# Order of 256- and 512-column products in an MLP's up blocks, and a last norm with a shorter root and paired stores

## The chip, the cores and the metric

One core of one Trainium2 chip. The metric is the device time of one execution in microseconds, as the median of several runs. The engines are TensorE (PE, with its weight loads shown as PEld), VectorE (DVE), ScalarE (ACT), GpSimd (POOL) and SyncE (SP), which mainly issues DMAs.

## The reference

One layer of a hybrid block over 512 latent tokens of width 2048 (with 256 context tokens ahead of the scans), all in float32. After two groups of recurrent heads and an output projection, the tokens pass through an RMSNorm, a SwiGLU MLP with a depthwise 3x3 convolution on its gate branch, a gated residual, and a final RMSNorm:

```
u = h @ w_up;  u_gate, u_val = split(u)          # 2048 -> 2 x 5504
g = conv3x3_depthwise(u_gate on an 8 x 64 grid) + conv_b
x = x + gt2 * ((silu(g) * u_val) @ w_down)       # 5504 -> 2048
out = x * rsqrt(mean(x*x) + eps) * g_final
```

## The kernel before, in words

Tokens lie in the free dimension (512 columns), channels in 128 partitions: x is 16 tiles of 128 x 512. Products at full accuracy are made of two float32r halves: a tensor is split into a high half (ScalarE casts, L90) and a low half (VectorE subtracts, L91), and high x high, high x low and low x high are added up in PSUM.

The MLP's 5504 channels are 43 tiles f of 128. The first four go through a plain product (up_two); the other 39 go through up_seven (L1207), which computes the two up products of a tile with seven block products in place of eight, a Strassen-like scheme over halves of the weights' 16 input tiles, gate and value, and left and right halves of the tokens. Each of the seven block products (product, L1226) has its own weight block, 128 x 1024, that is split into wh and wl, and eight input tiles k as operand, whose high and low halves of 256 tokens lie side by side. For each k there are two matmuls on TensorE: a **low product** of wl with the 256 columns of the operand's high half, and a **512-column product** of wh with both halves at once. In the kernel before, the eight low products of a block come first, and then the eight 512-column products:

```
for k in range(KH):
    mm(o[:, 0, :], wl[:, cs[k]], operands[n](k)[:, 0], start=first and k == 0, stop=False, ...)
for k in range(KH):
    mm(o, wh[:, cs[k]], operands[n](k), start=False, stop=k == KH - 1, ...)
```

The tiles wl rotate through two buffers (pool wlo), the tiles wh through three. The order of instructions on an engine follows the program order, except that the parts under tc.high_priority() are moved forward, the splits among them; each engine's queue is then worked off in order. Between the sixth and the seventh block product most tiles f also run one block of the down projection (down_block, L1298): 48 matmuls of 512 columns, whose result is added to x in DRAM by an accumulating DMA. Meanwhile VectorE and ScalarE do the splits, the sums of the scheme, and the convolution (nine taps, L1168 and L1170).

The end (from L1311): x is read back as 16 tiles x2[k]. For the first 12 of them the last down products are added (residual, L1041), the tile is squared (square, L1049, for the two parts of the tokens apart) and scaled by g_final on ScalarE (L1331). The last four tiles, k = 12 to 15, come by parts of the tokens: part 0 is tokens 0 to 383, part 1 is tokens 384 to 511. For each part: four down products, four residuals, four squares, then token_rstd (L1055): matmuls with a column of ones add up the squares over the channels (L1061), a mean with eps (L158) and rsqrt (L148) make 1/root on 128 x 3 or 128 x 1 numbers, and matmuls with the identity (L1068) spread them over all partitions into a PSUM tile r3, which ScalarE copies to SBUF as r3s (L1359). square adds the squares of several tiles on VectorE into one tile (L87), except for the last ones, which it keeps as tiles of their own (own): the last four where the part has 512 tokens (the norm behind the output projection), otherwise the last two. The small PSUM tiles of token_rstd come from a pool of two buffers (psB).

Finally, for each part and each k, x2[k] is multiplied by 1/root: k below 12 with k % 3 == 2 on GpSimd with r3s (L1369), the others on VectorE with r3, k of 12 and more with g_final in the same instruction (L1367). Each result is stored at once by a DMA of its own (L1373): part 0 from SP's queue, part 1 alternately from SP's and ScalarE's. The multiplications of part 1 have high priority.

token_rstd with rsqrt serves the norm behind the output projection too (four columns, before up_two).

Of the kernel before, what the change touches and what calls it, by code (L numbers as in the profile page):

```python
# [18 lines left out]
P = 128  # L19
D = 2048  # L20
# [50 lines left out]
def block_kernel(ctx: ExitStack, tc: tile.TileContext, a: dict, out: bass.AP):  # L71
# [11 lines left out]
    def mul(o, x, y):  # L83
        V.tensor_tensor(out=o, in0=x, in1=y, op=ALU.mult)
# [31 lines left out]
    msk = keep.tile([P, len(LEVELS), P], U8, name="msk")  # L116
    csil = keep.tile([P, 128], F32, name="csil")[:, 0:KT]
    modc = {n: keep.tile([P, KT], F32, name=f"mod{n}") for n in (2, 3, 4, 5)}
    wraw = pool(ctx, "wraw", 4)
    whi = pool(ctx, "whi", 2)  # L120
    wlo = pool(ctx, "wlo", 2)
# [26 lines left out]
    def rsqrt(v, t, o):  # L148

        S.activation(t, v, AF.Ln)  # L150
        S.activation(o, t, AF.Exp, scale=-0.5)
        mul(t, o, o)
        mul(t, t, v)
        V.tensor_scalar(out=t, in0=t, scalar1=-0.5, scalar2=1.5, op0=ALU.mult, op1=ALU.add)
        mul(o, o, t)

    def mean_eps(v, ps, n):
        V.tensor_scalar(out=v, in0=ps, scalar1=1.0 / n, scalar2=EPS, op0=ALU.mult, op1=ALU.add)  # L158
# [896 lines left out]
    def token_rstd(sums, pl, name, n=T):  # L1055

        nj = n // P
        ps = psb(f"ps_{name}", (P, nj))
        for i, sq in enumerate(sums):
            for j in range(nj):  # L1060
                PE.matmul(ps[:, j : j + 1], sq[:, P * j : P * j + P], cst[:, C_ONE : C_ONE + 1],  # L1061
                          start=(i == 0 and j == 0), stop=(i == len(sums) - 1), skip_group_check=True)
        var, scr, r = (pl.tile([P, nj], F32, name=f"{t}_{name}", tag=t) for t in ("rs1", "rs2", "rs3"))
        mean_eps(var, ps, D)
        rsqrt(var, scr, r)
        o = psb(f"rb_{name}", (P, n))
        for j in range(nj):
            PE.matmul(o[:, P * j : P * j + P], r[:, j : j + 1].to_broadcast([P, P]), ident, start=True, stop=True)  # L1068
        return o
# [137 lines left out]
    def up_seven(f):  # L1207
# [30 lines left out]
        def rows(x):  # L1238
# [103 lines left out]
    for pt, sl in enumerate(parts):  # L1342
        w = sl.stop - sl.start
        accs = [acc(f"dl{pt}_{i}", (P, w)) for i in range(4)]
        for i in range(4):
            c = slice(P * i, P * i + P)
            for n, (wh, wl, raw) in enumerate(wd):
                if pt == 0:
                    gh, gl = gs[fs[n]]
                    mm3(accs[i], wh[:, c], wl[:, c], gh[:, sl], gl[:, sl], n == 0, n == len(fs) - 1)  # L1350
                else:
                    mm(accs[i], raw[:, c], glast[:, n, :], start=(n == 0), stop=(n == len(fs) - 1))
        with tc.high_priority():
# [5 lines left out]
            S.copy(r3s, r3)  # L1359
        roots.append((r3, r3s))  # L1360
    for pt, sl in enumerate(parts):
        r3, r3s = roots[pt]
        with tc.high_priority() if pt else nullcontext():
            for k in range(KT):
                xx = x2[k][:, sl]
                if k >= 12:
                    V.scalar_tensor_tensor(out=xx, in0=xx, scalar=gnf[:, k : k + 1], in1=r3, op0=ALU.mult, op1=ALU.mult)  # L1367
                elif k % 3 == 2:
                    G.tensor_tensor(out=xx, in0=xx, in1=r3s, op=ALU.mult)  # L1369
# [3 lines left out]
                eng.dma_start(out[k, :, sl], xx)  # L1373


def arrange(x, c, ctx, c_ctx, w_mod, b_mod, g_norm1, g_norm2, w_in, gla_w_lr, gla_b_lr, mlstm_b_gate,
# [72 lines left out]
```

## Time and profile before

| what | value |
|---|---|
| median of 3 runs | 2485.04 us (2484.53 to 2485.16) |
| the profiled execution | 2483.26 us, of which the span is 2481.4 us |
| instructions | 35224 |
| TensorE busy | 98% of the span |
| VectorE, ScalarE, GpSimd busy | 71%, 45%, 15% |
| mean DMA rate | 173 GB/s |
| mean granted TensorE clock | 0.992 |

The profile is of one execution, so its own time stands beside the median. It has a page (busy time of the engines, shares of the chain of work that ended last, the costliest groups of instructions) and views that can be asked for a stretch: instructions in order of time, the chain in order of time, waits, DMAs, and busy time by stretches. In a row of the timeline the first number is the start in us from the span's beginning, the second the time that the group took; then come engine, line, operation, output<-input, shape and count, and in brackets the idle time of the engine before and what ended it. A row of the chain has start, time and what ran. A row of the stretches has the stretch, its length, busy time (and count) of PE, PEld, DVE, ACT and POOL, the granted clock, the DMA engines' share and GB/s. Matmuls are pipelined, and their ends are modelled, so two that follow one another overlap in the listing.

### The profile page before, as it was taken

What the parts mean: (1) busy time and instruction counts of PE and PEld (TensorE: products, weight loads), DVE (VectorE), ACT (ScalarE), POOL (GpSimd) and SP (SyncE); (2) the same over time, 40 slices, a digit from 0 to 9 for tenths busy, and PEclk for the clock granted to TensorE, in tenths of its full rate; (3) what the DMA queues carried; (4) which work ended last, traced back from release to release, by engine and by line L of the source; (5) the groups of instructions that cost most, each with busy time, mean ns of one, the idle gap of its engine ahead of it and who ended that gap; (6) DMA issues with size and microseconds to landing.
All of it is one profiled execution on the core that took longest, in us unless ns stands there. A gap on an engine that the chain in (4) does not pass through costs nothing.

```text
span 2481.4 us, 35224 instructions
## 1 busy us (share of the span) xinstructions
PE 2441.4 (98%) x13588; PEld 2107.1 (85%) x13588; DVE 1751.1 (71%) x2482; ACT 1113.2 (45%) x1652; POOL 367.4 (15%) x364
## 2 busy tenths in 40 slices
PE   7999999999999999999999999999999999999997
PEld 5888899888988888888888888888888888888886
DVE  5666766554545688777887777777777777777874
ACT  4224543322223444434455555555555555555552
POOL 0000000000000344540011111111111111111100
PEclk9999999999999999998999999999999999999998
DMA  9751012123433778862488888888888888888761
GB/s 380 270 190 57 33 38 78 63 93 125 136 132 102 266 267 293 280 196 90 144 187 191 192 191 198 193 191 192 190 193 188 187 193 190 191 190 191 177 202 68
DMA packets 138167, 429.66 MB, mean 173 GB/s; under 512 B 15760, under 2 KB 20240, under 8 KB 138000
## 3 DMA queue, kind: packets, MB, share of 16 engines
q1 hardware_dynamic: 104880, 348.24, 41.9%
q0 software_dynamic: 31968, 78.66, 19.7%
q8 instruction: 106, 1.74, 0.3%
q10 hardware_dynamic: 1152, 0.52, 0.1%
q14 instruction: 61, 0.50, 0.1%
HBM read 381.22 MB, written 46.14 MB: 172 GB/s over the span
## 4 chain that ended last, share of the span: by engine, by line
PE 95%; DVE 2%; DMA 1%; issue 1%; ACT 0%; SPq 0%; DVEq 0%; ACTq 0%
PE dn L98 18%; PE a L98 18%; PE x L98 17%; PE v L98 9%; PE wo L98 7%; PE ga L98 7%; PE w L98 4%; PE po L98 4%; PE u L98 4%; PE ps_m L98 1%; PE sl L98 1%; PE dl L98 1%; PE cst L98 1%; PE s L98 1%; PE mc L309 1%
## 5 line engine op out<-in xcount | busy, mean ns | idle before, releaser
L91 DVE TENSOR_TENSOR lo_q<-q,hi_q 128x1024 fp32r<-128x1024 f32 x195 | 235.4, 1223 | 142.6 <-ACT spare L1303 117.6
L90 ACT CAST hi_q<-q 128x1024 fp32r<-128x1024 f32 x195 | 205.2, 1052 | 230.0 <-PE dn L98 162.0
L98 PE MATMUL dn<-gh,lo_d 128*128 128x512 f32 x660 | 257.5, 390 | 0.0
L98 PE MATMUL dn<-gl,hi_d 128*128 128x512 f32 x660 | 257.5, 390 | 0.0
L98 PE MATMUL dn<-gh,hi_d 128*128 128x512 f32 x660 | 257.4, 390 | 0.0
L1170 DVE SCALAR_TENSOR_TENSOR cv<-pad,cwt,cv 128x512 f32<-128x512 f32 x328 | 246.7, 752 | 6.3 <-ACT cv L1168 0.5
L98 PE MATMUL x<-bt,hi_q 128*128 128x512 f32 x936 | 235.4, 394 | 0.0
L98 PEld LDWEIGHTS x<-bt,hi_q 128*128 128x128 f32 x936 | 167.6, 188 | 30.7
L1211 POOL DMA_DIRECT2D spare<-in_w_up x78 | 68.7, 884 | 720.0 <-DMA spare<-in_w_up 637.5
L298 POOL TENSOR_TENSOR sumg_m<-sumg_m,raw_m 128x512 f32<-128x512 f32 x74 | 124.1, 1677 | 199.3 <-ACT raw_m L297 170.7
L98 PE MATMUL a<-hi_h,hTh 128*128 128x256 f32 x512 | 150.3, 294 | 0.0
L91 DVE TENSOR_TENSOR lo_d<-raw_d,hi_d 128x1024 fp32r<-128x1024 f32 x84 | 101.3, 1206 | 65.8 <-ACT hi_d L90 51.4
L290 DVE SCALAR_TENSOR_TENSOR sum_m<-raw_m,csil,sum_m 128x512 f32<-128x512 f32 x112 | 145.5, 1299 | 1.3
L98 PEld LDWEIGHTS dn<-gl,hi_d 128*128 128x128 f32 x660 | 124.0, 188 | 26.2 <-DVE gl L91 0.2
L98 PEld LDWEIGHTS dn<-gh,hi_d 128*128 128x128 f32 x660 | 123.9, 188 | 26.3 <-ACT gh L90 0.4
L98 PEld LDWEIGHTS dn<-gh,lo_d 128*128 128x128 f32 x660 | 124.0, 188 | 26.0
L98 PE MATMUL a<-lo_h,hTh 128*128 128x256 f32 x512 | 144.9, 283 | 0.0
L98 PE MATMUL a<-hi_h,hTl 128*128 128x256 f32 x512 | 144.9, 283 | 0.0
L91 DVE TENSOR_TENSOR lo_q<-spare,hi_q 128x1024 fp32r<-128x1024 f32 x78 | 95.3, 1222 | 56.7 <-ACT hi_q L90 56.7
L98 PEld LDWEIGHTS x<-bt,lo_q 128*128 128x128 f32 x936 | 125.6, 188 | 10.3 <-ACT u L1277 1.1
L90 ACT CAST hi_h<-raw_h 128x1024 fp32r<-128x1024 f32 x64 | 67.0, 1048 | 138.3 <-PE a L98 131.2
L98 PE MATMUL x<-bt,lo_q 128*128 128x256 f32 x936 | 128.2, 279 | 0.7 <-ACT u L1277 0.7
(360 smaller groups left out, 5866.1 us busy)
## 6 DMA issues: line engine op xcount, KB each, us to landing
raw_m<-in_w_mod SPq DMA_DIRECT2D x192, 512.0 KB, 4.8
q<-in_w_up SPq DMA_DIRECT2D x117, 512.0 KB, 4.4
raw_d<-in_w_down SPq DMA_DIRECT2D x81, 512.0 KB, 3.5
spare<-in_w_up SPq DMA_DIRECT2D x78, 512.0 KB, 4.4
spare<-in_w_up POOLq DMA_DIRECT2D x78, 512.0 KB, 7.1
raw_h<-in_w_heads SPq DMA_DIRECT2D x64, 512.0 KB, 3.5
x2d<-stage POOLq DMA_DIRECT2D x72, 256.0 KB, 4.8
x2d<-spare POOLq DMA_DIRECT2D x72, 256.0 KB, 4.9
```

Source lines behind the costliest of these rows:

```text
L90: split_ins[0] = S.copy(hi, x).ins
L91: return V.tensor_tensor(out=lo, in0=x, in1=hi.bitcast(F32), op=ALU.subtract).ins
L98: ins = PE.matmul(*args, **kw)
L290: V.scalar_tensor_tensor(out=parts["v"], in0=raw[:, 0, :], scalar=ce, in1=parts["v"], op0=ALU.mult, op1=ALU.add)
L298: G.tensor_tensor(out=parts["g"], in0=parts["g"], in1=raw[:, 1, :], op=ALU.add)
L309: tc.keep_in_program_order(PE.matmul(ps[:, i : i + 1], po[:, P * i : P * i + P], cst[:, C_ONE : C_ONE + 1], start=True, stop=True))
L1170: V.scalar_tensor_tensor(out=t3, in0=src, scalar=w, in1=t3, op0=ALU.mult, op1=ALU.add)
L1211: eng.dma_start(q, a["w_up"][f - FIRST, i, j].rearrange("p k c -> p (k c)"), **kw)
```

## The change

Three edits. In up_seven the two loops over k become one, so that for each input tile k the low product and the 512-column product follow each other. token_rstd gets a new root: ScalarE takes the logarithm directly from the PSUM sums (with 1/n as its scale and eps as its bias), then the exponential, and VectorE refines the result in three instructions. At the end, the last four tiles are scaled by g_final on ScalarE behind their squares; part 1 keeps the squares of its last four tiles apart and spreads its 1/root into two PSUM tiles, one for VectorE and one for ScalarE's copy; x2 becomes one tile of 16 slices, and multiplications and stores take two slices at a time, in a written order of pairs n: four pairs of part 0 and two of part 1 on GpSimd, part 0's stores from SP's queue, part 1's four from SP's and four from ScalarE's. The DMAs of the stores keep the program's order.

```diff
+    epsc = keep.tile([P, 1], F32, name="epsc")
+    V.memset(epsc, EPS)
...
+    def root(o, total, n, t, v):
+
+        S.activation(t, total, AF.Ln, scale=1.0 / n, bias=epsc)
+        V.tensor_scalar(out=v, in0=total, scalar1=1.0 / n, scalar2=EPS, op0=ALU.mult, op1=ALU.add)
+        S.activation(o, t, AF.Exp, scale=-0.5)
+        if o.shape[1] == 1:
+            V.tensor_scalar(out=t, in0=o, scalar1=o, scalar2=-0.5, op0=ALU.mult, op1=ALU.mult)
+            V.tensor_scalar(out=t, in0=t, scalar1=v, scalar2=1.5, op0=ALU.mult, op1=ALU.add)
+            V.tensor_scalar(out=o, in0=o, scalar1=t, scalar2=None, op0=ALU.mult)
+            return
+        V.scalar_tensor_tensor(out=t, in0=o, scalar=-0.5, in1=o, op0=ALU.mult, op1=ALU.mult)
+        mul(t, t, v)
+        V.scalar_tensor_tensor(out=o, in0=t, scalar=1.5, in1=o, op0=ALU.add, op1=ALU.mult)
...
-        own = k >= KT - (4 if n == T else 2)
+        own = k >= KT - (2 if n == 3 * P else 4)
...
-        mean_eps(var, ps, D)
-        rsqrt(var, scr, r)
+        root(r, ps, D, scr, var)
+        if twice:
+            oo = [psb(f"rb_{name}{i}", (P, n)) for i in range(2)]
+            for o in oo:
+                PE.matmul(o, r.to_broadcast([P, P]), ident, start=True, stop=True)
+            return oo
...
             for k in range(KH):
                 mm(o[:, 0, :], wl[:, cs[k]], operands[n](k)[:, 0], start=first and k == 0, stop=False,
                    skip_group_check=True)
-            for k in range(KH):
                 mm(o, wh[:, cs[k]], operands[n](k), start=False, stop=k == KH - 1, skip_group_check=True)
...
-    x2 = [gp.tile([P, T], F32, name=f"x3_{k}") for k in range(KT)]
+    x3 = gp.tile([P, KT, T], F32, name="x3")
+    x2 = [x3[:, k, :] for k in range(KT)]
...
                 square(12 + i, sums3[pt], gp, f"fq{pt}", sl)
-            r3 = token_rstd(sums3[pt], gp, f"rmsf{pt}", w)
+                S.activation(x2[12 + i][:, sl], x2[12 + i][:, sl], AF.Copy, scale=gnf[:, 12 + i : 13 + i])
+            r3 = token_rstd(sums3[pt], gp, f"rmsf{pt}", w, pt == 1)
+            r3, r3b = r3 if pt else (r3, r3)
             r3s = gp.tile([P, w], F32, name=f"r3s{pt}", tag=f"r3s{pt}")
-            S.copy(r3s, r3)
+            S.copy(r3s, r3b)
...
-            for k in range(KT):
-                xx = x2[k][:, sl]
-                if k >= 12:
-                    V.scalar_tensor_tensor(out=xx, in0=xx, scalar=gnf[:, k : k + 1], in1=r3, op0=ALU.mult, op1=ALU.mult)
-                elif k % 3 == 2:
-                    G.tensor_tensor(out=xx, in0=xx, in1=r3s, op=ALU.mult)
+            for n in ((0, 1, 2, 3, 6, 5, 7, 4), (6, 7, 4, 0, 1, 5, 2, 3))[pt]:
+                ks = slice(2 * n, 2 * n + 2)
+                xx = x3[:, ks, sl]
+                if n in ((1, 4, 6, 7), (4, 5))[pt]:
+                    G.tensor_tensor(out=xx, in0=xx, in1=r3s.unsqueeze(1).to_broadcast([P, 2, w]), op=ALU.mult)
                 else:
-                    mul(xx, xx, r3)
-                eng = nc.scalar if pt and k % 2 else nc.sync
-                eng.dma_start(out[k, :, sl], xx)
+                    mul(xx, xx, r3.unsqueeze(1).to_broadcast([P, 2, w]))
+                eng = nc.scalar if pt and n in (7, 0, 5, 3) else nc.sync
+                tc.keep_in_program_order(eng.dma_start(out[ks, :, sl].rearrange("k p t -> p k t"), xx))
```

More of the change, by code (lines that the diff above doesn't have):

```diff
@@ L1053, in square, with token_rstd @@
             add(sums[0], sums[0], sq)
-    def token_rstd(sums, pl, name, n=T):
+    def token_rstd(sums, pl, name, n=T, twice=False):
         nj = n // P
@@ L1362, in block_kernel @@
         r3, r3s = roots[pt]
+        w = sl.stop - sl.start
         with tc.high_priority() if pt else nullcontext():
-            for k in range(KT):
-                xx = x2[k][:, sl]
-                if k >= 12:
-                    V.scalar_tensor_tensor(out=xx, in0=xx, scalar=gnf[:, k : k + 1], in1=r3, op0=ALU.mult, op1=ALU.mult)
-                elif k % 3 == 2:
-                    G.tensor_tensor(out=xx, in0=xx, in1=r3s, op=ALU.mult)
-                else:
-                    mul(xx, xx, r3)
-                eng = nc.scalar if pt and k % 2 else nc.sync
-                eng.dma_start(out[k, :, sl], xx)
+            for n in ((0, 1, 2, 3, 6, 5, 7, 4), (6, 7, 4, 0, 1, 5, 2, 3))[pt]:
[3 more added lines that the diff above has]
+                    G.tensor_tensor(out=xx, in0=xx, in1=r3s.unsqueeze(1).to_broadcast([P, 2, w]), op=ALU.mult)
+                else:
+                    mul(xx, xx, r3.unsqueeze(1).to_broadcast([P, 2, w]))
+                eng = nc.scalar if pt and n in (7, 0, 5, 3) else nc.sync
+                tc.keep_in_program_order(eng.dma_start(out[ks, :, sl].rearrange("k p t -> p k t"), xx))
 def arrange(x, c, ctx, c_ctx, w_mod, b_mod, g_norm1, g_norm2, w_in, gla_w_lr, gla_b_lr, mlstm_b_gate,
```

## The prediction

> **What bounds the kernel now.** I read the page first, then the chain of work that ended last, and then TensorE's instructions in order of time in the MLP, where two thirds of the span lie.
>
> ```profile
> span 2481.4 us, 35224 instructions
> PE 2441.4 (98%) x13588; PEld 2107.1 (85%) x13588; DVE 1751.1 (71%) x2482; ACT 1113.2 (45%) x1652; POOL 367.4 (15%) x364
> PE 95%; DVE 2%; DMA 1%; issue 1%; ACT 0%; SPq 0%; DVEq 0%; ACTq 0%
> ```
>
> TensorE carries 95% of the chain. The view of stretches over the MLP says how completely:
>
> ```profile
> 1170.00:2440.00 1270.00, 1269.33 (x6705) 1091.06 (x6704) 982.96 (x1243) 662.08 (x869) 200.00 (x229) 1.00 0.77 185
> ```
>
> and the view of waits, for TensorE over the same stretch, has a single row:
>
> ```profile
> PE x L98 <- ACT u L1277: 0.7, 1, 0.7
> ```
>
> In 1270 us TensorE waited 0.7 us, at granted clock 1.00. So in the MLP only two things can change the time: the pace at which matmuls follow one another, or a new wait. A listed duration is longer than the distance from start to start, because matmuls overlap, so I cost by starts. These are TensorE's rows over the time of one channel tile (the seventh block product of the tile before comes first): seven block products, each eight low matmuls of 256 columns and then eight of 512 (a pair, below, is one of each):
>
> ```profile
> 1623.89 1.11 PE L98 MATMUL x<-bt,lo_q 128*128 128x256 f32 x8
> 1624.83 2.04 PE L98 MATMUL x<-bt,hi_q 128*128 128x512 f32 x8
> 1626.70 1.10 PE L98 MATMUL x<-b,lo_q 128*128 128x256 f32 x8
> ...
> 1632.27 1.10 PE L98 MATMUL v<-bt,lo_q 128*128 128x256 f32 x8
> 1633.21 1.99 PE L98 MATMUL v<-bt,hi_q 128*128 128x512 f32 x8
> 1635.03 1.10 PE L98 MATMUL x<-bt,lo_q 128*128 128x256 f32 x8
> ...
> 1640.59 1.07 PE L98 MATMUL x<-bt,lo_q 128*128 128x256 f32 x8
> 1641.50 2.00 PE L98 MATMUL x<-bt,hi_q 128*128 128x512 f32 x8
> ```
>
> Low matmuls come every 0.94/8 = 117.5 ns (1632.27 to 1633.21), in the sixth block product (1640.59) every 0.91/8 = 114 ns. The 512-column matmuls right behind them come every 1.82/8 = 227.5 ns at best (1633.21 to 1635.03) and every 1.87/8 = 233.8 ns at worst (1624.83 to 1626.70). The chain gives the same tile in sums:
>
> ```profile
> 1624.05 5.60 PE x L98 x32
> 1629.65 2.78 PE w L98 x16
> 1632.43 2.76 PE v L98 x16
> 1635.20 2.78 PE x L98 x16
> 1637.98 2.78 PE v L98 x16
> 1640.76 2.75 PE x L98 x16
> 1643.50 10.89 PE dn L98 x48
> ```
>
> Seven block products take 5.60 + 2.78 + 2.76 + 2.78 + 2.78 + 2.75 = 19.45 us. The down block is an undisturbed run of 512-column matmuls: 10.89/48 = 226.9 ns each. So a long run settles at 226.9 ns, and a run of eight behind low ones pays up to 7 ns more for each. There are 39 channel tiles: 39 x 19.45 = 759 us stand under the first edit.
>
> **The change: the order of the matmuls.** Nothing is added or removed: a block product keeps its sixteen weight loads and eight pairs. Before there was one step from short to long in it; now there are eight. The trace of before has no such alternation, so it is bounded from both sides. Lower end: every matmul costs its best row, 114 + 226.9 = 340.9 ns a pair, 2.727 us a block product, 19.09 us a tile, 0.36 x 39 = 14 us less. Upper end: each 512-column matmul costs what one behind a low run costs at worst, 233.8 ns, and each low one 120 ns, the slowest steady pace that I find for 256 columns, in the early projection (23 starts in 2.76 us):
>
> ```profile
> 189.28 0.28 PE L98 MATMUL a<-lo_h,hTh 128*128 128x256 f32 x1
> ...
> 192.04 0.34 PE L98 MATMUL a<-hi_h,hch 128*128 128x384 f32 x1
> ```
>
> That is 353.8 ns a pair, 19.81 us a tile, 0.36 x 39 = 14 us more. I take the block product that now runs almost without surcharge, v<-bt with 2.76 us: 7 x 2.76 = 19.32, so 0.13 x 39 = 5.1 us less. The reason: what the seven differ by is a surcharge that dies out over the run that follows a switch, and a mixed stream has no long stretch of one kind in which loads and matmuls fall out of step. It is a choice, since the nearest rows, those behind a switch, lie on the other side.
>
> The order of instructions has one consequence for buffers. The low tile was free after its eight matmuls; now both tiles are read until the product's end, 1.82 us later. There are two low tiles, so the split two block products on (L91, VectorE) must wait. ScalarE's half (L90) already waits for a product's end, 0.78 us in the first of these rows:
>
> ```profile
> 1632.52 1.05 ACT L90 CAST hi_q<-q 128x1024 fp32r<-128x1024 f32 x1 [0.78 <-PE w L98]
> 1633.61 1.23 DVE L91 TENSOR_TENSOR lo_q<-q,hi_q 128x1024 fp32r<-128x1024 f32 x1
> ```
>
> The split at 1633.61 belongs to the product that starts at 1637.82 and reuses the tile of the product that runs from 1632.27 to 1635.03. It will start near 1635.05, end at 1636.3, and still be 1.5 us early. Behind it in VectorE's queue stand the adds that fill the padded image (L87) and the convolution's taps (L1170), for which TensorE does not wait soon. I take 0; the price if that cover is gone is a rival below.
>
> **The change: the last norm.** These are rows of the chain, first at the norm behind the output projection (the same root), then at the end:
>
> ```profile
> 1132.57 0.17 DVE rs_rms L158
> 1133.44 0.17 DVE rs_rms L84
> ...
> 2467.56 0.17 DVE rs_rmsf L158
> ...
> 2468.39 0.47 DVE x L84
> ...
> 2468.92 0.52 DVE x L1367
> ...
> 2469.51 0.52 DVE x L1367
> ...
> 2470.16 0.81 PE rb_rmsf L1068 x2
> 2470.99 0.27 ACT r3s L1359
> 2471.29 0.29 DVE x L84
> ```
>
> GpSimd's and SP's rows there, in order of time:
>
> ```profile
> 2462.59 3.92 POOL L1369 TENSOR_TENSOR x<-x,r3s 128x384 f32<-128x384 f32 x4 [67.45 <-ACT r3s L1359]
> 2463.62 14.56 SPq L1373 DMA_DIRECT2D out<-x  x24
> ```
>
> The second part's root starts at 2467.56 and VectorE multiplies at 2471.29, 3.73 us later. The shorter root takes the mean (0.17) and one of four small steps (0.17, as in the other norm) off that path; the second copy of the broadcast in a bank of its own lets VectorE start without waiting for ScalarE's copy (0.27); and three products of the first part, 0.47 + 0.52 + 0.52 = 1.51 us, sit between the small steps. By pairs the first part has four VectorE products of about 2 x 0.47 instead of twelve, so these three should be done earlier. Sum: 2.1 us. The other four pairs go to GpSimd, 2 x 3.92 = 7.8 us from about 2462.3 to 2470.1, just in time for its two pairs of the second part. Added are four scalings on ScalarE per part (beside TensorE's column sums), two more square tiles in those sums (instead of two VectorE adds) and one more broadcast of up to 0.4 us, on which only GpSimd's copy waits: TensorE has nothing else left there, so 0 each. That broadcast needs a second of the two small PSUM buffers, so it also waits for VectorE's last product of the first part.
>
> The stores then decide. Rows of the DMA view from 2463 to 2482 (40 slices of 0.475 us):
>
> ```profile
> GB/s 0 0 0 320 362 366 362 366 366 375 375 365 369 362 366 369 246 0 0 0 138 138 138 251 269 263 265 248 248 141 331 342 369 372 353 16 0 0 0 0
> out<-x SPq DMA_DIRECT2D x16, 192.0 KB, 2.1
> out<-x ACTq DMA_DIRECT2D x8, 64.0 KB, 1.8
> ```
>
> and SP's last wait:
>
> ```profile
> SPq L1439 <- DMA out<-x: 1.8, 1, 1.8
> ```
>
> SP's 24 issues end at 2463.62 + 14.56 = 2478.18, 1.8 us later the last bytes are reported, and the program closes at 2481.4. Bytes flow from 2464.4 to 2479.6, with a hole of 1.4 us and a thin stretch behind it. By pairs SP has twelve issues and ScalarE four, so the issues (0.5 us each) stop being the limit. The bytes remain: 16 x 192 KB at 366 GB/s is 8.6 us, 16 x 64 KB at 257 GB/s (the slices of 251 to 248) is 4.1 us. The first root is 0.33 us shorter too, so the flow starts near 2464.0 and ends at 2476.7: 3.0 us less. Bounds: 1.5 us less if three pair products of 0.9 us still stand between the root's steps; 4.2 us less if the small rows flow at 366. The Trainium skill (DMA: Bandwidth & Descriptors, Issuing engines are not separate DMA queues) says that DMAs of all issuing engines share the same 16 DMA engines, so that issuing from several saves issue time only. The trace agrees: with two queues issuing the rate is 257, not more than 366 GB/s.
>
> In the norm behind the output projection TensorE is idle until the root is done; its two steps go with their gaps: 0.4 us. Together 3.4 us for the norms and 5.1 us for the order: 8.5 us. The profiled execution took 2483.26 us (its span and 1.86 us around it), 1.78 us under the median of 2485.04; the same difference gives 2476.5.
>
> **The rivals.** *Order is nothing*: a matmul costs by its columns whatever stands before it. For it: five of the seven block products on the chain lie within 2.75 to 2.80 us although they use different tiles. Only the norms count: 2485.04 - 3.4 = 2481.6. [...]
>
> *Floor*: each load of a low tile's weights now has a long matmul to hide under, and all pairs settle at 340.9 ns: 14 + 3.4 = 17.4 us less, 2467.6. For it: the sixth block product runs its low ones at 114 ns. Against it: a load for the 512-column matmul still falls into the short one.
>
> *Switching costs* (slower): each switch pays. For it: the 512-column matmuls behind a low run are the slowest of the trace. It decides for slower where a pair costs more than 347.3 ns (19.45/56) by over 1.6 ns (3.4 us over 39 x 56 pairs), which uses up the norms' gain. At the upper end, 353.8 ns, it is 14 - 3.4 = 10.6 us more, 2495.6; with 233.8 and 117.5 ns it is 0.22 x 39 - 3.4 = 5.2 us more, 2490.2.
>
> *Low tile too late* (slower): if VectorE's split misses its block product, TensorE stands still. From the rows it decides only when the split slips 1.5 us more; half a microsecond in two of seven would be 39 us, 35.6 with the norms, 2520.6.
>
> **How the numbers follow.** Forecast 0.42, order is nothing 0.24, floor 0.16, switching 0.14, low tile 0.04. Likeliest: 2476.5. From 2466 (floor with the norms' best bound, 14 + 4.2 + 0.4) to 2490 (switching at its milder price) all but the rest of switching and the late tile, under 0.2, are inside. A measurement of this kernel can tell about 0.2%, 5.0 us, from no change. Faster by more: forecast and floor less the forecast's bad end (norms 1.5 us, order half), with a little of order is nothing at its best bound: 0.60. Within 0.2%: 0.26. Slower: 0.14.
>
> **What would show it.** In the profile after: seven products in 19.3 us on the chain, TensorE's wait row still under 2 us, VectorE's first product of the second part about 2.1 us earlier against the last product of the down projection, and no hole in the row of bytes. A pair at 353 ns, a wait of TensorE for VectorE's split, or a hole of bytes between the parts would prove me wrong, each in its own step.

## The result, and the profile after

| kernel | median | runs | ratio to before, 95% interval |
|---|---|---|---|
| before | 2484.47 us (2482.91 to 2485.38) | 16 | |
| after | 2489.67 us (2487.59 to 2491.72) | 16 | 1.0023 (1.0016 to 1.0030) |

The change makes the kernel slower by 5.2 us. The prediction had 2476.5 us, faster. The profiled execution after has a span of 2487.7 us, 6.3 us more than before's 2481.4.

First the page, and the stretch of the MLP with the same columns as before (stretch, length, busy time and count of PE, PEld, DVE, ACT, POOL, granted clock, DMA share, GB/s):

```profile
span 2487.7 us, 35192 instructions
PE 2449.0 (98%) x13594; PEld 2109.1 (85%) x13594; DVE 1759.6 (71%) x2464; ACT 1110.4 (45%) x1660; POOL 370.7 (15%) x362
```

```profile
1170.00:2440.00 1270.00, 1268.33 (x6666) 1086.86 (x6665) 993.61 (x1240) 654.14 (x868) 200.30 (x229) 1.00 0.78 185
```

TensorE is as full as it was, at the same granted clock of 1.00, but the trace has 6666 matmuls in this time where it had 6705 before. That is the loss: the stream has become slower, not interrupted. The view of TensorE's waits in the MLP says the same. Here are all its rows (total, times, longest):

```profile
PE x L98 <- DVE lo_q L91: 1.2, 1, 1.2
PE dn L98 <- DVE lo_d L91: 0.4, 1, 0.4
```

Two waits for a low half, once each, 1.6 us against 0.7 before; all three fall into the first of the 39 channel tiles. The chain in order of time shows the pace (start, us, what; the tile that the prediction took apart):

```profile
1627.31 5.63 PE x L98 x32
1632.94 2.83 PE w L98 x16
1635.77 2.81 PE v L98 x16
1638.58 2.79 PE x L98 x16
1641.37 2.79 PE v L98 x16
1644.16 2.80 PE x L98 x16
1646.96 10.89 PE dn L98 x48
```

The seven block products take 19.65 us instead of 19.45, while the down block keeps its 10.89. Over 39 tiles that is 0.20 x 39 = 7.8 us, and with the 0.9 us of additional waits 8.7 us. On the chain the first product of the last down block (dl) starts 2449.54 - 2440.85 = 8.7 us later. The MLP's first product had come 1139.63 - 1139.07 = 0.6 us earlier, behind the changed norm, so the MLP lost 9.3 us in all; the 0.6 us that the two terms leave are not traced. The rows of before and of after:

```profile
2440.85 9.25 PE dl L98 x53
...
2466.03 0.34 PE dl L98 x2
```

```profile
2449.54 9.25 PE dl L98 x53
...
2472.32 2.35 PE dl L98 x20
...
2475.86 0.27 ACT rs_rmsf L161
2476.15 0.21 ACT rs_rmsf L163
...
2476.39 0.22 DVE rs_rmsf L165
...
2476.64 0.23 DVE rs_rmsf L166
...
2476.89 0.23 DVE rs_rmsf L167
...
2477.25 0.47 PE rb_rmsf L1084 x2
...
2477.74 0.42 DVE x L84
```

From there on the changed kernel is the faster one: from the start of dl to the program's end it takes 2487.7 - 2449.54 = 38.2 us instead of 2481.4 - 2440.85 = 40.6 us, 2.4 us less. The root of the second part is six rows without a stranger between them: 2475.86 to 2477.74 is 1.9 us instead of 3.7. The row of bytes (40 slices of 0.675 us from 2463 to 2490) has no hole any more, and the stores come in fewer, larger pieces:

```profile
GB/s 0 0 0 0 0 0 0 0 24 0 0 0 0 0 0 234 364 366 366 364 355 376 362 353 360 355 325 341 350 272 288 286 288 220 2 0 0 0 0 12
...
out<-x SPq DMA_DIRECT2D x8, 384.0 KB, 3.8
out<-x ACTq DMA_DIRECT2D x4, 128.0 KB, 4.4
out<-x SPq DMA_DIRECT2D x4, 128.0 KB, 3.1
```

Bytes flow from 2463 + 15 x 0.675 = 2473.1 to 2463 + 34 x 0.675 = 2486.0, 12.9 us in one piece; before it was 15.2 us with the hole. A part of the gain is missing at the start of this flow. VectorE's and SP's rows there:

```profile
2471.19 0.35 DVE L1057 SCALAR_TENSOR_TENSOR x<-dl,mod,x 128x128 f32<-128x128 f32 x1 [1.92 <-PE dl L98]
2471.45 1.81 DVE L84 TENSOR_TENSOR x<-x,rb_rmsf 128x768 f32<-128x768 f32 x2
```

```profile
2472.43 12.04 SPq L1395 DMA_DIRECT2D out<-x  x12
```

VectorE's first product of the first part stands in its queue behind a residual that waits for TensorE, and a product by pairs takes 0.9 us (1.81 for two) before its store can be issued.

### The profile page after: what moved, and what is told of

Same layout as the page of the kernel before. It is cut to its first block, busy times and chain, and to the rows that moved or that the text cites. A ratio compares the mean times of both kernels' runs of the same rounds, so it can differ in the third digit from the quotient of the medians.

```text
span 2487.7 us, 35192 instructions
## 1 busy us (share of the span) xinstructions
PE 2449.0 (98%) x13594; PEld 2109.1 (85%) x13594; DVE 1759.6 (71%) x2464; ACT 1110.4 (45%) x1660; POOL 370.7 (15%) x362
## 4 chain that ended last, share of the span: by engine, by line
PE 95%; DVE 3%; DMA 1%; issue 1%; ACT 0%; SPq 0%; DVEq 0%; ACTq 0%
PE dn L98 18%; PE a L98 18%; PE x L98 17%; PE v L98 9%; PE wo L98 7%; PE ga L98 7%; PE w L98 4%; PE u L98 4%; PE po L98 4%; PE ps_m L98 1%; PE sl L98 1%; PE dl L98 1%; PE cst L98 1%; PE s L98 1%; PE mc L325 1%
## 5 line engine op out<-in xcount | busy, mean ns | idle before, releaser
L98 PE MATMUL x<-bt,hi_q 128*128 128x512 f32 x936 | 332.9, 395 | 0.0
L98 PE MATMUL x<-bt,lo_q 128*128 128x256 f32 x936 | 262.2, 280 | 1.2 <-DVE lo_q L91 1.2
L98 PEld LDWEIGHTS x<-bt,hi_q 128*128 128x128 f32 x936 | 176.0, 188 | 40.8
L98 PEld LDWEIGHTS x<-bt,lo_q 128*128 128x128 f32 x936 | 175.9, 188 | 2.9 <-ACT u L1296 1.5
```

Of the source, the lines that this page charges most:

```text
L98: ins = PE.matmul(*args, **kw)
```

## The experiments

Time of a tile below is the sum of its seven block products on the chain, as in the fence above; the mean block product is worked out from the starts of all block products of up_seven in the trace, some of which contain a wait. Eight pairs make a block product. The theories, with the letters of the expectations: **A**, a surcharge on the matmuls behind a switch that dies out over the run; **S**, a fixed price for each switch of width; **B**, the low tile that is split too late; **O**, the layout of the operand's halves in SBUF; **L**, the pace of the matmuls falls into repeating patterns that depend on the sequence of widths and carry a state on. The first two and B are rivals of one another for the whole loss; O and L came up after the first runs.

| kernel | tile, us | mean block product, ns | median, us | ratio to before, 95% interval |
|---|---|---|---|---|
| before | 19.45 | 2782.7 | 2484.47 | |
| after | 19.65 | 2813.2 | 2489.67 | 1.0023 (1.0016 to 1.0030) |
| e1_norms | 19.45 | 2782.7 | 2480.26 | 0.9986 (0.9977 to 0.9995) |
| e2_order | 19.65 | 2813.0 | 2492.13 | 1.0031 (1.0020 to 1.0043) |
| e4_groups4 | 19.55 | 2795.4 | 2486.31 | 1.0010 (1.0001 to 1.0019) |
| e5_snake | 19.46 | 2781.7 | 2483.02 | 0.9994 (0.9985 to 1.0003) |
| e3_groups2 | 19.36 | 2773.0 | 2481.67 | 0.9988 (0.9979 to 0.9997) |
| e8_flat | 19.45 | 2782.7 | 2484.08 | 1.0001 (0.9992 to 1.0010) |
| e9_norms_flat | 19.45 | 2782.7 | 2481.31 | 0.9990 (0.9981 to 0.9999) |
| e10_norms_groups2 | 19.36 | 2773.1 | 2478.34 | 0.9979 (0.9970 to 0.9988) |
| e13_norms_groups2_wide_first | 19.36 | 2770.5 | 2479.08 | 0.9980 (0.9972 to 0.9989) |
| e14_norms_groups332 | 19.53 | 2795.8 | 2485.63 | 1.0010 (1.0001 to 1.0018) |
| e15_norms_groups62 | 19.43 | 2783.9 | 2483.68 | 0.9999 (0.9990 to 1.0008) |

Before was measured anew beside each group of kernels, with medians between 2483.33 and 2484.56 us, and each ratio is to the one beside it. Three more kernels, e7_wide, e11_half_alt and e12_half_runs, were run once each, for their traces.

### Each part alone

e1_norms is the kernel after with the old order of the products; e2_order is the kernel before with the alternation alone.

```diff
 # e1_norms, against after
                 mm(o[:, 0, :], wl[:, cs[k]], operands[n](k)[:, 0], start=first and k == 0, stop=False,
                    skip_group_check=True)
+            for k in range(KH):
                 mm(o, wh[:, cs[k]], operands[n](k), start=False, stop=k == KH - 1, skip_group_check=True)
 # e2_order, against before: the same line removed
```

> The changed kernel with the old order of matmuls in the up blocks (eight low ones, then eight of 512 columns); both norms and the stores as changed. Every theory of the order expects block products of 2.78 us as before. From the two profiles: the second part of the last norm is 2.4 us shorter from the last down block to the end (38.2 for 40.6 us) and the root behind the output projection about 0.3 us: 2.5 to 3 us under the kernel before. If the 5 us that the change lost came from the norms' new waits (SP waits 2.5 us for earlier stores there), this kernel would be slower than before, by about as much as the change.

> The kernel before with the alternation alone. Theory A, a change of width between neighbours costs time and the surcharge dies out over the run behind it: block products of 2.81 us on average in place of 2.78, 273 of them, 8 us slower. Theory B, the low tile that is freed late: the same total, but as waits of TensorE for VectorE's splits and not as longer steps from start to start; TensorE's waits in the MLP would add up to 8 us.

Measured: the norms alone bring 2484.56 - 2480.26 = 4.3 us, the order alone costs 2492.13 - 2484.56 = 7.6 us. Of the 4.3 us the two profiles account for the 2.5 to 3 that were expected; the interval holds both. The two make -4.3 + 7.6 = 3.3 us, beside the change's 5.2, which the intervals allow (1.2 to 5.7 us less, 5.0 to 10.7 us more). e2_order has the tile of 19.65 us of the kernel after, and its two waits of 1.2 and 0.4 us. So the whole loss belongs to the order, and B is out as its cause: the late low tile costs 1.6 us at most, where 7.6 are to be explained.

### Fewer and more switches

In e4_groups4 and e3_groups2 four, or two, low products are followed by the 512-column products of the same input tiles, so that there are two, or four, steps from short to long in a block product, where before has one and after eight. e5_snake keeps runs of eight, but in three of seven block products puts the 512-column products first, so that equal widths meet where one block product follows another and there are fewer switches than before.

```diff
 # e3_groups2, against before (e4_groups4: 4 for 2)
-            for k in range(KH):
-                mm(o[:, 0, :], wl[:, cs[k]], ...)
-            for k in range(KH):
-                mm(o, wh[:, cs[k]], ...)
+            for g in range(0, KH, 2):
+                for k in range(g, g + 2):
+                    mm(o[:, 0, :], wl[:, cs[k]], ...)
+                for k in range(g, g + 2):
+                    mm(o, wh[:, cs[k]], ...)
 # e5_snake, against before; low and both are the two loops
+            at = place[0] % 7
+            place[0] += 1
+            for i, part in enumerate((both, low) if at in (1, 3, 6) else (low, both)):
+                part(first and i == 0, i == 1)
```

> The kernel before with groups of four: four low matmuls, four of 512 columns, twice per block product, two switches from short to long in place of one. Theory A (the surcharge of a 512-column matmul goes by its place behind the switch; from before, 234, 233, 229, 230 ns, then 228 to 229): 2.794 us a block product, 3 us slower than before. Theory S (every switch costs the same, as the change's eight switches against one say, 30 ns over seven): 4.3 ns a block product, 1.2 us slower. Theory B: nearly as bad as the full alternation, since the low tile is read until six matmuls before the end, 6 to 8 us slower.

> The kernel before with the two halves of a block product in turned order in three of seven (512 columns first, then low ones), so that equal widths meet across block products and a tile has four switches from short to long in place of seven, three of them behind low runs of sixteen. Theory A: the surcharge of 28 ns per block product over its settled 2.755 us falls by 3/7, 12 ns times 273, 3.3 us faster. Theory S: 3/7 of 4.3 ns, 0.5 us faster. If width has nothing to do with it, 0.

> The kernel before with groups of two (two low matmuls, two of 512 columns, four switches per block product). Groups of four measured 2.795 us a block product, 12.7 ns over before for one switch more, full alternation 2.813, 30 ns over for seven more. Theory S, a price per switch taken from groups of four: 38 ns over before, 2.82 us, 10 us slower. Theory L, matmuls and weight loads lock into repeating patterns that depend on the spacing and not on the number of switches: anywhere between 2.78 and 2.83 us, with durations that repeat every two or three pairs inside a block product.

Measured: groups of four lose 0.0010. A has its 2.794 us a block product (2795.4 ns); S had 4.3 ns for the one switch more, and 12.7 are measured, but the time still goes up with the switches. Groups of two end that: with four steps from short to long they are faster than before with its one, 2773.0 against 2782.7 ns. A fixed price per switch has no room for this, and neither has a surcharge that every switch renews. The snake, with fewer switches, is not told apart from before, and its block product (2781.7 ns) lacks the 12 ns less that A expected. So A and S fall both: the number of switches does not decide.

What the traces show instead is that the single distances repeat. TensorE's rows at the start of such a product in e3_groups2:

```profile
1630.19 0.40 PE L98 MATMUL w<-b,lo_q 128*128 128x256 f32 x2
1630.43 0.62 PE L98 MATMUL w<-b,hi_q 128*128 128x512 f32 x2
1630.89 0.39 PE L98 MATMUL w<-b,lo_q 128*128 128x256 f32 x2
1631.12 0.62 PE L98 MATMUL w<-b,hi_q 128*128 128x512 f32 x2
1631.57 0.40 PE L98 MATMUL w<-b,lo_q 128*128 128x256 f32 x2
```

From start to start that is 0.24, 0.46, 0.23 and 0.45 us. By single matmuls the sixteen distances of four of the seven block products are, in ns, 120, 118, 229, 232, 113, 113, 226, 229 and the same again. In after's first two block products of a tile they are 118, 235, 118, 231, 117, 233, 123, 237 and so on round. And a long run of one width has steps too: in before the eight 512-column products of w end 226, 229, 232, 226, 229. The median of each place over the 39 tiles is the same in before, e1_norms and e8_flat to about 1 ns. This is what theory L expects.

The other three block products show other sequences for the same widths, and what sets them apart is a thing that none of the theories names: the buffer of the high weights. Every third tile wh lies in another pool than the other two (hi_tile, L179). A down block takes two such tiles itself, so in a tile f with a down block the third buffer holds the weights of the third block product (v<-bt), the sixth and the seventh. In before the 512-column products of the third and the sixth settle at 226 to 227 ns (2764 and 2746 ns a block product), while the first, second, fourth and fifth go on with 226, 229, 232 (2778 to 2787). Three of the last four tiles run no down block before their seventh product. There the third buffer falls to other products, and the pattern goes with the buffer. Before's chain in one of these tiles, from the second product on:

```profile
2347.12 2.75 PE w L98 x16
2349.87 2.78 PE x L98 x16
2352.65 2.78 PE v L98 x16
2355.43 2.75 PE x L98 x16
```

Here the second and the fifth have the third buffer and are the short ones, and v<-bt, with one of the other two, takes 2.78 us instead of 2.76. In e3_groups2, the first tile aside, the 111 products with the third buffer take 2769 to 2777 ns and the 155 others 2758 to 2760, without an exception. No run changed the buffers alone, so this is read from the traces and not tested.

### Width, and the operand's layout

e7_wide is the alternation with low products of 512 columns as well; its pace counts, not its time. In before the operand's two halves of an input tile do not lie next to one another in memory, as the words on the kernel suggest, but at least 8 KB apart; e8_flat lays them side by side in five of seven block products, so that the 512 columns are one contiguous stretch; e9_norms_flat is that with the new norms and the old order.

```diff
 # e7_wide, against e2_order
-                mm(o[:, 0, :], wl[:, cs[k]], operands[n](k)[:, 0], ...)
+                mm(o, wl[:, cs[k]], operands[n](k), ...)
 # e8_flat, against before (and what reads them)
-    b0t = [bp.tile([P, 2, KH, TH], F32R, ...
+    b0t = [bp.tile([P, KH, 2, TH], F32R, ...
-    btt = [bp.tile([P, 2, KH, TH], F32R, ...
+    btt = [bp.tile([P, KH, 2, TH], F32R, ...
```

> The kernel before with the alternation, and the low matmuls too with 512 columns (they add the product of the two low halves, which the other kernels leave out), so that the weights alternate between two tiles and the width is always 512. If the mix of widths costs: all 512-column matmuls at 227 ns, as in the down block, a block product 3.63 us. If the alternation of the weight tiles, or the operand, costs: 229 to 235 ns, 3.66 to 3.76 us. Either way some 235 us slower than before; the pace counts, not the total.

> The kernel before with the high and low halves of each operand tile side by side (five of seven block products: the 512 columns are one run of 512 in place of two runs of 256 that lie 8 KB apart). Theory O, the operand's two runs cost: the 512-column matmuls of these five settle at 227 ns as in the down block and not in the repeating 226, 229, 232; some 2 ns times 8 times 195 block products, 3 us faster. Theory A or L (width alone, or the spacing of loads): no change, within 1 us.

> The changed kernel with the old order of matmuls and with the halves side by side. The norms alone measured 4.3 us under the kernel before; with theory O 7 us under it, otherwise the same 4.3 us.

Measured: e7_wide took 2725.92 us in its one run; its block product of sixteen 512-column matmuls takes 3673.8 ns, 229.6 each. That lies in the range expected if the alternation of the weight tiles, or the operand, costs, and not at 3.63 us. In most of the products with the two ordinary buffers the steps repeat 226, 229 and 232; in those with the third buffer, and right behind them, they lie between 225 and 241. So neither those three steps nor the longer ones need a change of width. The alternation of the tiles wl and wh with every matmul costs at most 229.6 - 226.9 = 2.7 ns against the down block's pace. The layout does nothing: e8_flat has the same 2782.7 ns and the same distances place by place, so O is out. e9_norms_flat repeats the gain of the norms: 2.7 us against before's 2484.00.

### The load of the weights

In e11_half_alt (alternation) and e12_half_runs (old order) the weights of all input tiles of a block product but the first have 64 columns instead of 128. If the load has a part in the pace, the block product gets shorter; if the widths alone set it, it stays. Each kernel ran once.

```diff
 # e11_half_alt, against e2_order; e12_half_runs has the two loops of before
+            def one(k, wt, ob, rhs, **kw):
+                p = slice(0, P if k == 0 else P // 2)
+                mm(ob[p], wt[:, P * k : P * k + p.stop], rhs, skip_group_check=True, **kw)
```

> The kernel before with the alternation and, from the second input tile on, weights of 64 columns in place of 128, so that half of the up products' output channels get only the first input tile's part (the rest is left out). The widths that stream, 256 and 512, stay. [...] Theory S or A, widths alone: pairs stay at 347 to 352 ns.

> The same half weights in the old order, eight low ones and then eight of 512 columns (the same part left out). Theory L: low ones at 113 ns or less, 512-column ones at 220 to 227, without the repeating 226, 229, 232, and the same pair as in the alternation, so that the order has become nothing. Theory S or A: 2.78 us a block product, 30 ns under the alternation with half weights.

The view of weight loads by shape (busy time, mean ns of one, idle time before), first of after, then of e11_half_alt:

```profile
L98 PEld LDWEIGHTS x<-bt,lo_q 128*128 128x128 f32 x32 | 6.0, 188 | 0.1
```

```profile
L98 PEld LDWEIGHTS x<-bt,lo_q 128*64 128x64 f32 x28 | 3.7, 134 | 0.0
```

A half load is listed with 134 instead of 188 ns. The mean block product falls from 2813.0 to 2774.8 ns with alternation and from 2782.7 to 2757.0 in the old order; the price of the alternation falls from 30.3 to 17.8 ns. The widths that stream are the same, so the widths alone do not set the pace. Half as many weight columns also mean half as many output partitions for each matmul, and the two runs do not part the one from the other; that it is the load is argued, not shown. Nor is it the whole cause: a pair still takes 2774.8/8 = 346.9 ns with alternation, at the edge of the 347 to 352 of S and A, and 2757.0/8 = 344.6 in the old order, where L had 113 and at most 227, together 340; steps of 226, 229, 232 remain in the old order, and the order still counts, though L expected it to become nothing. The Trainium skill (TensorE: Matmul & The Clock Gate, Back-to-back issue gap) says that in a stream of loads and matmuls both set the spacing. These two runs agree with it, by 38.2 and 25.7 ns less a block product, as far as they part the load from the rest. Its figure of about 131 ns for a 512-column matmul in such a stream does not hold for this kernel's float32r products: the down block takes 10.89/48 = 226.9 ns each.

### Groups of two with the norms

e10_norms_groups2 joins the two parts that were faster: the kernel after with groups of two. e13_norms_groups2_wide_first has the two 512-column products first in each group.

```diff
 # e10_norms_groups2, against after: the loops of e3_groups2
 # e13_norms_groups2_wide_first
+            for g in range(0, KH, 2):
+                for k in range(g, g + 2):
+                    mm(o, wh[:, cs[k]], operands[n](k), start=first and k == 0, stop=False, ...)
+                for k in range(g, g + 2):
+                    mm(o[:, 0, :], wl[:, cs[k]], operands[n](k)[:, 0], start=False, stop=k == KH - 1, ...)
```

> The changed kernel with groups of two in place of the full alternation. If the two effects add up: groups of two alone were 2.3 to 2.9 us under the kernel before (ratio 0.9988), the norms alone 3.5 to 4.3 us; together 6 to 7 us under it, about 2478. Block products of 2.77 us, with pairs of low matmuls at 113 and 113 or 120 and 118 ns in turn.

> The same with the 512-column matmuls first in each group of two. Theory L (the pattern of widths sets the pace): across block products the sequence is the same two and two, so 2.77 us a block product and 6 to 7 us under the kernel before. Theory A or S (a price at each switch): as well, since the number of switches is the same. If the buffers matter: a little slower, since the high tile, which is split first, is needed as early as before and the low one later.

Measured: 2478.34 us against 2484.05, ratio 0.9979 (0.9970 to 0.9988), faster than before and after. The effects add up: 4.3 us of the norms and 2.3 of the groups alone (2484.00 - 2481.67) make 6.6, measured are 5.7. The chain of one tile:

```profile
1622.98 5.54 PE x L98 x32
1628.52 2.76 PE w L98 x16
1631.28 2.77 PE v L98 x16
1634.06 2.76 PE x L98 x16
1636.82 2.76 PE v L98 x16
1639.58 2.77 PE x L98 x16
1642.35 10.91 PE dn L98 x48
```

Seven block products in 19.36 us, 0.09 under before. That it is better than the norms alone is shown by the pace, 273 x (2782.7 - 2773.1) ns = 2.6 us, of which 0.02 x 36 = 0.7 us go back, since the down block, which 36 tiles have, takes 10.91 instead of 10.89 us; the intervals of the two ratios overlap. Wide first is the same within what the runs can tell.

### A rule for the pattern, put to the test

In most rows of the traces up to here low products in runs or pairs went at 113 ns behind a 512-column product of 232 ns, and at 118 behind one of 226 or 229. If a group holds a whole cycle of three, each could end on 232. e14_norms_groups332 has groups of three, three and two, e15_norms_groups62 of six and two.

```diff
 # e14_norms_groups332, against e10_norms_groups2 (e15_norms_groups62: ((0, 6), (6, KH)))
-            for g in range(0, KH, 2):
-                for k in range(g, g + 2):
+            for g, h in ((0, 3), (3, 6), (6, KH)):
+                for k in range(g, h):
```

> The kernel after, with groups of three, three and two (three low products, three 512-column products, three low, three 512-column, two low, two 512-column). Theory L (the pace falls into a repeating pattern with a state that is carried on): in the traces so far undisturbed 512-column products repeat 226, 229, 232 ns, and low ones run at 113 ns behind a 232 and at 118 behind a 226 or 229. Three 512-column products are one whole cycle, so if the cycle starts at 226 in each group, every group of three ends on a 232 and its followers are low products at 113: 2 x (3 x 113 + 687) + 2 x 113 to 118 + 455 to 461 = 2733 to 2751 ns a block product, 273 x 22 to 40 ns = 6 to 11 us less than with groups of two (2773.1 ns), median 2468 to 2473 us. If the cycle starts elsewhere (233, 236, 229 behind low ones at 118, as in the groups of four) it is up to 2 x (354 + 698) + 699 = 2803 ns, 8 us more than with groups of two. Rival F (only the number of switches counts, with a best near groups of two): between groups of two and the kernel before, 2773 to 2783 ns, median 2478 to 2481 us.

> The kernel after, with groups of six and two (six low products, six 512-column products, two low, two 512-column). Theory L: six 512-column products are two whole cycles of 226, 229, 232 ns, so at best six low ones at 113 with 1374 ns, and a group of two at 681 to 699: 2733 to 2751 ns a block product, median 2468 to 2473 us; out of step, with low ones at 118 and 233, 236 first, 708 + 1389 + 699 = 2796 ns, median 2485 us. Rival F (number of switches alone): two switches lie between one (2782.7 ns) and four (2773.1 ns), near 2780 ns, median 2480 us.

TensorE's rows in e15_norms_groups62, in order of time:

```profile
1631.89 0.84 PE L98 MATMUL w<-b,lo_q 128*128 128x256 f32 x6
1632.57 1.53 PE L98 MATMUL w<-b,hi_q 128*128 128x512 f32 x6
1633.94 0.39 PE L98 MATMUL w<-b,lo_q 128*128 128x256 f32 x2
1634.17 0.62 PE L98 MATMUL w<-b,hi_q 128*128 128x512 f32 x2
1634.62 0.87 PE L98 MATMUL v<-bt,lo_q 128*128 128x256 f32 x6
1635.33 0.88 PE L98 MATMUL v<-bt,hi_q 128*128 128x512 f32 x3
```

The product w has its six low ones at (1632.57 - 1631.89)/6 = 113 ns and takes 1634.62 - 1631.89 = 2.73 us, the best of the expectation. But its last two 512-column products leave v to start at (1635.33 - 1634.62)/6 = 118 ns; v takes 2.80 us on the chain. Two of the seven block products get the good pattern, the others do not, and the mean is 2783.9 ns. In e14_norms_groups332 the two patterns mix likewise, 2.76 and 2.80 us, with a mean of 2795.8 ns. So F falls with e14: three steps from short to long are slower than both one and four. L holds insofar as the pattern that it foretold appears to the nanosecond, and as equal sequences inside a block product take different times by what came before them, which is a carried state. The buffer alone does not explain it: the products with weights in one of the two ordinary buffers take 2735 ns in the tiles f = 5 to 40 and 2792 in 41 and 42. But it did not foretell which phase comes up, and the hoped-for 2468 to 2473 us did not come. In e14 the rule has an exception too: behind 236, 232 the low ones ran at 119, 117, 117 in three of the seven block products, those with the third buffer. The exception was already there in before, where the seventh block product ends with 236, 232 and the next one starts with 119 and 117 or 118.

Both kernels lose more than the mean says: e15_norms_groups62 is level with before although it has the new norms and nearly before's block product. Its down block takes 10.93 instead of 10.89 us on the chain, 1.4 us over the 36 tiles that have one, and TensorE waits once for 1.4 us, 0.7 more than before; with the 0.3 us of its mean (273 x 1.2 ns) that is 2.4 of the 4.3 us of the norms. The rest is inside the intervals.

## Why the prediction was wrong

**What bounds the kernel** was right: TensorE's pace in the MLP, not a wait, decided. The stretch that was read is half of the span (1270 of 2481.4 us), not two thirds; no term of the sum hangs on that.

**The order of the matmuls** is the step that failed, in its sign. The prediction took -5.1 us, with the block product v<-bt of 2.76 us for all seven, because "a mixed stream has no long stretch of one kind in which loads and matmuls fall out of step". Measured are 19.65 us a tile, 7.8 us more on the chain and 7.6 by the runs of e2_order. The bounds of 14 us either way held it, and a pair takes 19.65/56 = 350.9 ns, almost the 351.3 of the rival *Switching costs* at its milder price. Its price for the two parts, 233.8 and 117.5 ns, lies close to what the trace has: on the mean over all block products the 512-column products went from 230.5 to 233.0 ns and the low ones from 117.3 to 118.7. The rows quoted for the forecast already spoke against it: the 512-column products behind a low run were the slowest. The reason was the wrong one, not only the choice: it needed a surcharge that dies out over a run and that an alternation does not renew. In v<-bt the surcharge does die out (233 and 231 ns, then 226 to 227), but that goes with the buffer of its high weights, and with the same buffer the alternation takes 2799 to 2806 ns a block product. Groups of two and the snake show that neither a surcharge renewed at each switch nor a price per switch sets the time. Being near the rival's number does not make the rival's mechanism right either, for groups of two switch four times as often as before and are faster.

**The late low tile** was taken as 0 and the waits of the MLP are 0.9 us longer than before, all of it in the first of the 39 tiles. The step was right in kind: VectorE's split does wait for the product's end now, and misses its block product in one case only.

**The last norm** was right in direction, and its size nearly so: 3.4 us predicted for the norms together, 4.3 by e1_norms, whose interval (0.9977 to 0.9995 of 2484.5, or 5.7 to 1.2 us) holds it. By steps: the norm behind the output projection was given 0.4 us. Its rows after:

```profile
1130.78 1.55 PE ps_rms L1077 x8
...
1132.36 0.27 ACT rs_rms L161
...
1132.65 0.21 ACT rs_rms L163
...
1133.59 2.06 PE rb_rms L1088 x8
```

From the end of the sums at 1132.33 to the broadcast it is 1.26 us, where before had 1.60: 0.3 us. The second part's VectorE products were to come 2.1 us earlier against the last dl: they stand 2477.74 - 2474.67 = 3.1 us behind its end instead of 2471.29 - 2466.37 = 4.9, so 1.8 earlier. The end was to come 3.0 us earlier and came 2.4 earlier. The flow of bytes has the length foretold (12.9 against 12.7 us), but the prediction let it start 0.4 us earlier against the last dl. It started later: SP's first issue stood 2466.37 - 2463.62 = 2.75 us ahead of the end of dl before, and 2474.67 - 2472.43 = 2.24 after, since the first product of a pair takes 0.9 us and waits behind a residual. That is the 0.9 us between forecast and trace; 0.4 us came back because the last down block itself took 2474.67 - 2449.54 = 25.1 instead of 25.5 us. One new wait was not foreseen: SP now waits for earlier stores to land, in its waits from 2470 to 2488:

```profile
SPq L1395 <- DMA out<-x: 2.5, 2, 1.3
```

It costs nothing that the row of bytes shows, since the rate stays at 325 to 376 GB/s through it.

**The chances.** *Order is nothing* had half of it: the norms' 2481.6 is close to what e1_norms does (2480.26), but order is not nothing. *Floor*, 340.9 ns a pair, is not reached by any order tried; the best, groups of two, takes 19.36/56 = 345.7. Shown are that the order alone costs the time, that it costs it through the pace and not through waits, and that neither the number of switches, nor the operand's layout, nor a low tile that comes late explains it. Shown too that the widths are not all: with half the weight columns the same widths go faster, and in the traces, without a run of its own, the pattern goes with the buffer of the high weights. What stays open is what sets the pattern that a sequence of widths locks into; a change of the buffers alone, another length of load between 64 and 128 columns, or a long stream of one pattern with nothing before it, was not tried.

## What to carry to other kernels

Where TensorE never waits, a change of the matmuls' order is a change of pace of some ns each, and times thousands this is all that counts: 3.6 ns a pair here outweigh the whole gain of a shortened end. Such a pace cannot be had from durations of another order, nor from the one product that looks best, which here had its weights in another buffer than most; measure the order by itself, and try several groupings (here two and two was best, one and one worst) before any reason is believed. And when two independent edits come in one change, time each alone: here a good one of 4.3 us was buried under a bad one of 7.6.

## What the runs showed of the hardware

- The distances between matmuls that never wait repeat to about 1 ns place by place between kernels with the same order (before, e1_norms, e8_flat), and come mostly in few values: 113, 118, 120 and 123 ns for 256 columns, 226, 229, 232 and up to 241 for 512, at granted clock 1.00.
- The same sequence inside a block product takes 2735 or 2790 ns (medians over the tiles, e15_norms_groups62) by what ran before it.
- The same sequence takes 2769 to 2777 ns with the high weights in the third buffer and 2758 to 2760 with them in the other two (e3_groups2, the first tile aside; read from the trace, not tested by a change of the buffers).
- The 512-column matmuls show the cycle 226, 229, 232 even where no other width is near (e7_wide, 229.6 on the mean), in most of the products with the two ordinary buffers.
- Halving the columns of the weights shortens the listed load from 188 to 134 ns and the block product by 26 to 38 ns of 2783 to 2813, though no load stood on the path by any wait that the profile lists.
- Stores with rows of 512 bytes (the second part, 128 tokens) flow at 272 to 288 GB/s, those of 1536 bytes (384 tokens) at up to 376.
